# Sums of up-projection weights on VectorE in place of adding DMAs, in a one-core hybrid encoder layer

## The chip, the core and the metric

The kernel runs on one core of one Trainium2 chip. Times are device microseconds (us) of one execution; lower is better. A core has TensorE (PE) for matmuls, VectorE (DVE), ScalarE (ACT), GpSimd (POOL), which here issues DMAs that add into their destination, and SyncE (SP), which issues the plain loads. Each of these works through its own list of instructions in order, and semaphores hold an instruction back until what it needs is there.

## What is computed

One post-norm layer on x of 512 x 1024 floats: a token-mixing part (state-space branch, dilated attention, gates) and a channel part. The change lies in the channel part:

```
h = layer_norm(alpha * h + mix, ln1_g, ln1_b)
f = jnp.square(jax.nn.relu(h @ w_up)) @ w_down      # w_up 1024 x 4096, w_down 4096 x 1024
h = layer_norm(alpha * h + f, ln2_g, ln2_b)
```

## The kernel before

Every fp32 matmul is done as three matmuls on split operands: a high part (a cast to fp32r by ACT) and a low part (the source minus the high part, by DVE). So each block of weights passes from HBM into a raw tile, then ACT writes its high part, then DVE its low part, and PE multiplies.

The channel part has 32 column blocks of `w_up`, each 128 columns wide, in four chunks of eight, and `w_down` is consumed by chunk. The first eight blocks are done plainly. The other 24 are done as **12 pairs**, numbered n = 0 to 11 (`PAIRS`, line 1029), while the down projection of the chunk before is multiplied between them. The big loop at line 1265 has three **passes**, c = 0, 1, 2, of four pairs each (n = 4c + q) and seven products of the down projection. A pair is a Strassen-like scheme with seven instead of eight quarter products; it needs sums of weights. The pair's two blocks lie in raw tiles r0 and r1 (named `pr`, three buffers in the tag `wraw`, which SP loads). K0 and K1 are the halves of a tile's 1024 columns. `pair_prep(n, e)` makes the operands in four steps:

- e = 0, operand tile pa: r0 as it stands (two quarter products, into the PSUM banks x and y);
- e = 1, operand tile pb: T1 = r0K0 + r1K0 and T2 = T1 + r1K1, kept in the two halves of pb (banks z and x);
- e = 2, operand tile pc: r1, whose K0 half has become r1K0 + r1K1 (banks x and z);
- e = 3, operand tile pd: r0K1 + T2 (bank x).

The four sums are made in place in r0 and r1, by four adding DMAs of 256 KB that POOL issues (lines 1063, 1067, 1068, 1070). pa, pb, pc and pd rotate through three slots (`slot`), two of them in one tag and one in another; so pa of the next pair waits until PE has done with this pair's pb. `pair_load` for r1 of pair n + 1 is issued once r1 of pair n has had its last reader, which is the low part of pc; r0 likewise after pd.

PE's order is written by hand (`manual_schedule`, lines 1264 to 1300). Within a pair it is: x and y from pa, then z and x from pb, then x and z from pc, then x from pd, twelve matmuls each. The products of the down projection stand between them, 24 matmuls each, named `ps_p` by line 148 to 150. For the first pair of a pass (q = 0) pb follows pa at once. For the others half a product stands between pa and pb, and its other half between pb and pc:

```
if q == 0:
    up_seg(n, 1)
    pair_prep(n, 3)
pr = product(c, SEQ[2 * q], ops)
next(pr)
if q:
    up_seg(n, 1)
    pair_prep(n, 3)
```

The operands of a product are ah, al (the activations) and ch, cl (the weights, two tiles each, in two buffers per tag). The down weights are summed too, by four adding DMAs of 1 MB per pass (`wq<-wq`, line 1171), which POOL issues from the same list. The one that the second pair of a pass needs (its first product, `SEQ[2]`) starts only when the operands of the product before have been split, since it adds into the tile that they were split from.

The order on ACT, DVE, POOL and SP isn't written by hand: a list scheduler sets it when the program is built, from the dependences and its own costs. So the order after the change is that scheduler's, too.

Of the kernel before, what the change touches and what calls it, by code (L numbers as in the profile page):

```python
# [13 lines left out]
ALU = mybir.AluOpType  # L14
# [26 lines left out]
def f32(ap):  # L41
    return ap.bitcast(F32)
# [3 lines left out]
def hybrid_layer_kernel(ctx: ExitStack, tc: tile.TileContext, t: dict, out: bass.AP):  # L46
    nc = tc.nc
    act, dve, pool, pe, dma = nc.scalar, nc.vector, nc.gpsimd, nc.tensor, nc.sync
# [984 lines left out]
    def pair_load(n, j):  # L1033
        if n < len(PAIRS):
            ch, b = PAIRS[n]
            raw_w[n, j] = wp.tile([P, 1024], F32, name=f"pr{n}_{j}", tag="wraw", bufs=3)
            dma.dma_start(raw_w[n, j], t["w_up"][ch * 8 + b + j])
# [3 lines left out]
    def slot(name):  # L1041
        s_ = slot_n[0] % 3
        slot_n[0] += 1
        if s_ < 2:
            return [wp.tile([P, 1024], F32R, name=f"{name}{x}", tag=f"w{x}", bufs=2) for x in "hl"]
        return [fp.tile([P, 1024], F32R, name=f"{name}{x}", tag=f"x{x}", bufs=1) for x in "hl"]

    def wsplit(h, l, src):
        act.copy(h, src)
        dve.tensor_sub(l, src, f32(h))  # L1050

    K0, K1 = slice(0, 512), slice(512, 1024)

    def pair_prep(n, e):

        if n >= len(PAIRS):
            return
        r0, r1 = raw_w[n, 0], raw_w.get((n, 1))
        if e == 0:
            h, l = slot(f"pa{n}")  # L1060
            wsplit(h, l, r0)
            op_w[n, "B11"], op_w[n, "B21"] = (h, l, K0), (h, l, K1)
            pool.dma_start(r0[:, K0], r1[:, K0], accum_op=ALU.add)
        elif e == 1:
            h, l = slot(f"pb{n}")
            wsplit(h[:, K0], l[:, K0], r0[:, K0])
            pool.dma_start(r1[:, K0], r1[:, K1], accum_op=ALU.add)
            pool.dma_start(r0[:, K0], r1[:, K1], accum_op=ALU.add)
            wsplit(h[:, K1], l[:, K1], r0[:, K0])
            pool.dma_start(r0[:, K1], r0[:, K0], accum_op=ALU.add)  # L1070
            op_w[n, "T1"], op_w[n, "T2"] = (h, l, K0), (h, l, K1)
        elif e == 2:
            h, l = slot(f"pc{n}")
            wsplit(h, l, r1)
            op_w[n, "T3"], op_w[n, "B22"] = (h, l, K0), (h, l, K1)
            pair_load(n + 1, 1)
        else:
            h, l = slot(f"pd{n}")
            wsplit(h[:, K0], l[:, K0], r0[:, K1])
            op_w[n, "T4"] = (h, l, K0)  # L1080
            pair_load(n + 2, 0)
# [162 lines left out]
    for b in range(NU, 8):  # L1244
        if b == 4:
            hf_ctx.close()
            qp = wq_ctx.enter_context(tc.tile_pool(name="qp", bufs=1, side="right", reuse_waits="tile"))
            load_quarters(0)
        up_block(0, b)
        if b == 2:  # L1250
            s3 = act_sums()
        if b == 7:
            act_split("S3", s3)
            pair_load(0, 0)
            pair_load(0, 1)
            pair_load(1, 0)
            pair_prep(0, 0)
            pair_prep(0, 1)
# [5 lines left out]
    with tc.manual_schedule(engines={mybir.EngineType.PE}):  # L1264
        for c in range(3):
            for q in range(4):
                n = c * 4 + q
                if q:
                    up_seg(n - 1, 3)
                up_seg(n, 0)  # L1270
                pair_prep(n, 2)
                if q == 0:
                    up_seg(n, 1)
# [148 lines left out]
```

## Time and profile before

| | us |
|---|---|
| median of 3 timed runs (1026.52 to 1027.15) | 1026.8 |
| the profiled execution's own time | 1027.21 |
| its span, first to last instruction | 1025.4 |
| PE busy, share of the span | 991.2, 97% |
| DVE busy | 758.8, 74% |
| ACT busy | 589.8, 58% |
| POOL busy | 103.0, 10% |
| mean granted TensorE clock, of 1 | 0.985 |

The profile names an instruction by its line in the kernel, its engine, its operation and the tiles that it writes and reads (`out<-in`). In a timeline the first column is the start, the second the time from the first start to the last end, `xN` the number of instructions merged, and what stands in brackets is the idle time of the engine just before and what ended it. The time between the starts of two instructions that follow each other without a wait is a little shorter than one instruction's duration, as the next one enters while the last one drains. In a table of stretches, `PEclk` is the clock that TensorE was granted. PE's busy time is an average over the whole kernel: 97% says that few microseconds are without a matmul, not that the matmuls ran at full clock.

### The profile page before, as it was taken

What the parts mean: (1) busy time and instruction counts of PE and PEld (TensorE: products, weight loads), DVE (VectorE), ACT (ScalarE), POOL (GpSimd) and SP (SyncE); (2) the same over time, 40 slices, a digit from 0 to 9 for tenths busy, and PEclk for the clock granted to TensorE, in tenths of its full rate; (3) what the DMA queues carried; (4) which work ended last, traced back from release to release, by engine and by line L of the source; (5) the groups of instructions that cost most, each with busy time, mean ns of one, the idle gap of its engine ahead of it and who ended that gap; (6) DMA issues with size and microseconds to landing.
All of it is one profiled execution on the core that took longest, in us unless ns stands there. A gap on an engine that the chain in (4) does not pass through costs nothing.

```text
span 1025.4 us, 14690 instructions
## 1 busy us (share of the span) xinstructions
PE 991.2 (97%) x5399; PEld 841.0 (82%) x5399; DVE 758.8 (74%) x1176; ACT 589.8 (58%) x1127; POOL 103.0 (10%) x110
## 2 busy tenths in 40 slices
PE   9999999999999999999999999998999799789997
PEld 7888888888887887788788888887898689679986
DVE  4396998689988998984984483964885777668756
ACT  4454795579757975965763443364655456455630
POOL 0000100110021003011000000001212211221100
PEclk9999999999999999999999999999999899889999
DMA  6445475226633772665752386066777886875522
GB/s 237 149 143 151 130 219 186 93 98 197 195 107 106 223 212 76 200 194 169 262 155 90 104 272 231 23 206 143 151 209 186 178 191 180 194 160 135 136 92 82
DMA packets 61992, 165.67 MB, mean 162 GB/s; under 512 B 8032, under 2 KB 9312, under 8 KB 60128
## 3 DMA queue, kind: packets, MB, share of 16 engines
q1 hardware_dynamic: 53136, 139.30, 42.2%
q0 software_dynamic: 8640, 25.17, 13.4%
q8 instruction: 42, 0.69, 0.3%
q10 hardware_dynamic: 144, 0.26, 0.1%
q14 instruction: 30, 0.25, 0.1%
HBM read 128.25 MB, written 11.30 MB: 136 GB/s over the span
## 4 chain that ended last, share of the span: by engine, by line
PE 75%; DMA 12%; DVE 6%; issue 4%; ACT 2%; POOL 1%; SPq 0%; DVEq 0%; POOLq 0%; ACTq 0%
PE ps_pa L138 9%; PE ps_z L138 9%; PE ps_x L138 9%; PE ps_g L138 7%; DMA pr<-pr 6%; DMA wq<-wq 4%; PE ps_q L138 3%; PE ps_k L138 3%; PE ps_x L1089 2%; PE ps_u L138 2%; PE ps_B L138 2%; PE ps_yo L529 2%; PE ps_C L138 2%; DMA pr<-in_w_up_dram 2%; PE ps_p L149 1%
## 5 line engine op out<-in xcount | busy, mean ns | idle before, releaser
L108 DVE TENSOR_TENSOR wl<-wraw,wh 128x1024 fp32r<-128x1024 f32 (+1 forms) x117 | 144.1, 1236 | 104.8 <-ACT wh L107 79.5
L107 ACT CAST wh<-wraw 128x1024 fp32r<-128x1024 f32 (+1 forms) x117 | 120.9, 1037 | 105.7 <-PE ps_vb L150 16.5
L148 PE MATMUL ps_p<-ch,ah 128*128 128x512 f32 x168 | 67.8, 404 | 3.0 <-ACT ch L1183 3.0
L149 PE MATMUL ps_p<-cl,ah 128*128 128x512 f32 x168 | 68.0, 405 | 2.6 <-DVE cl L1184 2.6
L1184 DVE TENSOR_TENSOR cl<-wq,ch 128x1024 fp32r<-128x1024 f32 x42 | 51.0, 1221 | 22.4 <-ACT ch L1183 22.4
L150 PE MATMUL ps_p<-ch,al 128*128 128x512 f32 x168 | 67.0, 399 | 0.0
L1183 ACT CAST ch<-wq 128x1024 fp32r<-128x1024 f32 x42 | 43.4, 1043 | 16.2 <-DMA wq<-wq 10.1
L138 PE MATMUL ps_pa<-yh,wh 128*128 128x512 f32 x128 | 51.7, 404 | 0.0
L138 PE MATMUL ps_g<-xh,wh 128*128 128x512 f32 x128 | 51.5, 402 | 0.0
L138 PE MATMUL ps_z<-xh,wh 128*128 128x512 f32 x128 | 50.7, 396 | 0.0
L138 PE MATMUL ps_x<-xh,wh 128*128 128x512 f32 x128 | 50.5, 394 | 0.0
L138 PE MATMUL ps_z<-xl,wh 128*128 128x512 f32 x128 | 49.9, 390 | 0.0
L138 PE MATMUL ps_g<-xl,wh 128*128 128x512 f32 x128 | 49.9, 390 | 0.0
L138 PE MATMUL ps_x<-xl,wh 128*128 128x512 f32 x128 | 49.9, 390 | 0.0
L498 ACT ACTIVATE U<-bc,acr 128x128 f32<-128x128 f32 x128 | 42.4, 391 | 11.1 <-DMA bc<-dr_acr 7.5
L138 PE MATMUL ps_pa<-yl,wh 128*128 128x512 f32 x128 | 48.4, 393 | 0.0
L317 DVE SCALAR_TENSOR_TENSOR acc<-ps_x,vec,acc 128x510 f32<-128x510 f32 (+1 forms) x64 | 47.6, 743 | 0.8 <-ACT acc L315 0.3
L500 DVE SCALAR_TENSOR_TENSOR U<-bc,acr,U 128x128 f32<-128x128 f32 x128 | 42.0, 364 | 0.6 <-ACT U L498 0.6
L138 PE MATMUL ps_u<-ht,wh 128*128 128x512 f32 (+1 forms) x160 | 41.7, 348 | 0.2 <-ACT ht L955 0.2
L504 ACT ACTIVATE G<-cb,tok 128x128 f32<-128x128 f32 x128 | 41.8, 391 | 0.0
L148 PEld LDWEIGHTS ps_p<-ch,ah 128*128 128x128 f32 x168 | 32.9, 196 | 9.8 <-ACT ch L1183 3.7
L149 PEld LDWEIGHTS ps_p<-cl,ah 128*128 128x128 f32 x168 | 32.8, 195 | 9.7 <-DVE cl L1184 3.9
(752 smaller groups left out, 2679.9 us busy)
## 6 DMA issues: line engine op xcount, KB each, us to landing
wraw<-in_w_in_dram SPq DMA_DIRECT2D x68, 512.0 KB, 3.6
bc<-dr_acr SPq DMA_DIRECT2D x64, 256.0 KB, 4.6
wq<-in_w_dn_dram SPq DMA_DIRECT2D x24, 512.0 KB, 4.7
wq<-wq POOLq DMA_DIRECT2D x12, 1024.0 KB, 7.9
pr<-in_w_up_dram SPq DMA_DIRECT2D x24, 512.0 KB, 4.9
pr<-pr POOLq DMA_DIRECT2D x48, 256.0 KB, 3.5
be<-dr_ear SPq DMA_DIRECT2D x32, 256.0 KB, 5.4
wraw<-in_w_ps_dram SPq DMA_DIRECT2D x16, 512.0 KB, 3.7
```

What stands on the lines that cost most here:

```text
L107: act.copy(h[:, :width], r[:, :width])
L108: dve.tensor_sub(l[:, :width], r[:, :width], f32(h[:, :width]))
L138: ins = pe.matmul(ps, l, r, start=(first and n == 0), stop=(last and n == len(seq) - 1))
L148: pe.matmul(ps, lh, rh, start=(first and i == 0), stop=False)
L149: pe.matmul(ps, lh, rl, start=False, stop=False)
L150: ins = pe.matmul(ps, ll, rh, start=False, stop=(last and i == n - 1))
L317: dve.scalar_tensor_tensor(acc[:, o0:o1], ps[:, i0:i1], w(k), acc[:, o0:o1], op0=ALU.mult, op1=ALU.add)
L498: act.activation(U[:, ch(c)], bb[:, ch(c)], AF.Identity, bias=acr[:, c, 32 + h:33 + h])
L500: dve.scalar_tensor_tensor(U[:, ch(c)], bf[:, ch(c)], acr[:, c, h:h + 1], U[:, ch(c)], op0=ALU.subtract, op1=ALU.min)
L504: act.activation(G1[:, ch(c)], cb[0][:, c, :], AF.Copy, scale=tok[:, c, h:h + 1])
L1183: act.copy(h, w[:, j, :])
L1184: dve.tensor_sub(l, w[:, j, :], f32(h))
```

## The change

The four adding DMAs of a pair become four VectorE additions of 128 x 512 floats, in place, on the same halves; and the split of pb, which called `wsplit` for each half, is written out so that the additions stand between the casts and the subtractions. Loads, matmuls, the adding DMAs of the down weights and the order on PE stay as they are.

```
         if e == 0:
             h, l = slot(f"pa{n}")
             wsplit(h, l, r0)
             op_w[n, "B11"], op_w[n, "B21"] = (h, l, K0), (h, l, K1)
-            pool.dma_start(r0[:, K0], r1[:, K0], accum_op=ALU.add)
         elif e == 1:
             h, l = slot(f"pb{n}")
-            wsplit(h[:, K0], l[:, K0], r0[:, K0])
-            pool.dma_start(r1[:, K0], r1[:, K1], accum_op=ALU.add)
-            pool.dma_start(r0[:, K0], r1[:, K1], accum_op=ALU.add)
-            wsplit(h[:, K1], l[:, K1], r0[:, K0])
-            pool.dma_start(r0[:, K1], r0[:, K0], accum_op=ALU.add)
+            dve.tensor_add(r0[:, K0], r0[:, K0], r1[:, K0])
+            act.copy(h[:, K0], r0[:, K0])
+            dve.tensor_add(r1[:, K0], r1[:, K0], r1[:, K1])
+            dve.tensor_sub(l[:, K0], r0[:, K0], f32(h[:, K0]))
+            dve.tensor_add(r0[:, K0], r0[:, K0], r1[:, K1])
+            act.copy(h[:, K1], r0[:, K0])
+            dve.tensor_add(r0[:, K1], r0[:, K1], r0[:, K0])
+            dve.tensor_sub(l[:, K1], r0[:, K0], f32(h[:, K1]))
             op_w[n, "T1"], op_w[n, "T2"] = (h, l, K0), (h, l, K1)
```

The first place is DVE's list at pair 0, the first pair of the first pass. `pa0`, `pb0` and `pc0` are its operands (h the high part, l the low part), `pr_0` and `pr_1` its raw tiles; line 1015 splits activations, line 1169 (now 1171) sums activations for the down projection, line 1178 (now 1180) splits them, and line 1120 (now 1122) takes bank y out of PSUM. Before:

```order
L1050 TENSOR_TENSOR pa0l<-pr_0_6741,pa0h 128x1024
L1015 TENSOR_TENSOR ht<-s_6553,ht 128x4x256
L1050 TENSOR_TENSOR pb0l<-pr_0_6741,pb0h 128x512
L1169 TENSOR_TENSOR r_0_6470<-r_0_6470,r_1_6616 128x4x256
L1120 TENSOR_TENSOR r_1_6777<-ps_y_6791,v_0_6804 128x256
L1050 TENSOR_TENSOR pc0l<-pr_1_6743,pc0h 128x1024
L1178 TENSOR_TENSOR al_6882<-r_0_6470,ah_6881 128x1024
L1050 TENSOR_TENSOR pb0l<-pr_0_6741,pb0h 128x512
```

And of the change, at the same place on DVE:

```order
L1050 TENSOR_TENSOR pa0l<-pr_0_6741,pa0h 128x1024
L1065 TENSOR_TENSOR pr_0_6741<-pr_0_6741,pr_1_6743 128x512
L1067 TENSOR_TENSOR pr_1_6743<-pr_1_6743 128x512
L1015 TENSOR_TENSOR ht<-s_6553,ht 128x4x256
L1050 TENSOR_TENSOR pc0l<-pr_1_6743,pc0h 128x1024
L1068 TENSOR_TENSOR pb0l<-pr_0_6741,pb0h 128x512
L1171 TENSOR_TENSOR r_0_6470<-r_0_6470,r_1_6616 128x4x256
L1069 TENSOR_TENSOR pr_0_6741<-pr_0_6741,pr_1_6743 128x512
L1122 TENSOR_TENSOR r_1_6777<-ps_y_6791,v_0_6804 128x256
L1071 TENSOR_TENSOR pr_0_6741<-pr_0_6741 128x512
L1180 TENSOR_TENSOR al_6882<-r_0_6470,ah_6881 128x1024
L1072 TENSOR_TENSOR pb0l<-pr_0_6741,pb0h 128x512
```

The four additions (L1065, L1067, L1069, L1071) stand between the splits, and the split of pc has moved ahead of both halves of pb.

The second place is DVE's list in the second pair of the second pass (pair 5), from its pc to the second half of the next product's weights, `cl_7927`. `pr_0_7669` and `pr_1_7851` are the raw tiles of pair 6, `v` and `h` are sums of the output. Before:

```order
L1050 TENSOR_TENSOR pc5l<-pr_1_7634,pc5h 128x1024
L1050 TENSOR_TENSOR pd5l<-pr_0_7501,pd5h 128x512
L1184 TENSOR_TENSOR cl_7923<-wq_01_7553,ch_7922 128x1024
L1050 TENSOR_TENSOR pa6l<-pr_0_7669,pa6h 128x1024
L1234 TENSOR_TENSOR v_0_7697<-v_0_7697,ps_p_3_7853 128x512
L1223 TENSOR_TENSOR h_0_6038<-h_0_6038,v_0_7697 128x512
L1234 TENSOR_TENSOR v_1_7700<-v_1_7700,ps_p_4_7854 128x512
L1178 TENSOR_TENSOR al_7997<-r_0_7209,ah_7996 128x1024
L1223 TENSOR_TENSOR h_1_6039<-h_1_6039,v_1_7700 128x512
L1184 TENSOR_TENSOR cl_7927<-wq_01_7553,ch_7926 128x1024
```

And of the change:

```order
L1050 TENSOR_TENSOR pc5l<-pr_1_7634,pc5h 128x1024
L1050 TENSOR_TENSOR pd5l<-pr_0_7501,pd5h 128x512
L1180 TENSOR_TENSOR al_7919<-r_0_7209,ah_7918 128x1024
L1186 TENSOR_TENSOR cl_7923<-wq_01_7552,ch_7922 128x1024
L1050 TENSOR_TENSOR pa6l<-pr_0_7669,pa6h 128x1024
L1236 TENSOR_TENSOR v_0_7697<-v_0_7697,ps_p_3_7853 128x512
L1065 TENSOR_TENSOR pr_0_7669<-pr_0_7669,pr_1_7851 128x512
L1225 TENSOR_TENSOR h_0_6038<-h_0_6038,v_0_7697 128x512
L1236 TENSOR_TENSOR v_1_7700<-v_1_7700,ps_p_4_7854 128x512
L1137 SCALAR_TENSOR_TENSOR r_1_7599<-ps_x_7817,v_5_7892 128x256
L1225 TENSOR_TENSOR h_1_6039<-h_1_6039,v_1_7700 128x512
L1186 TENSOR_TENSOR cl_7927<-wq_01_7552,ch_7926 128x1024
```

L1065, the first sum of pair 6, which reads the raw tile `pr_1_7851`, now stands in DVE's list ahead of `cl_7927`. The first and third pass have L1065 of pairs 2 and 10 at the same place.

The third place is POOL's list at pair 4, the first pair of the second pass. Before:

```order
L1063 DMA pr_0_7293<-pr_1_7452 128x512
L1067 DMA pr_1_7452<-pr_1_7452 128x512
L1171 DMA wq_00_7550<-wq_01_7553 128x2048
L1068 DMA pr_0_7293<-pr_1_7452 128x512
L1171 DMA wq_01_7553<-wq_11_7556 128x2048
L1070 DMA pr_0_7293<-pr_0_7293 128x512
```

And of the change, where nothing but adding DMAs of the down weights is left from here to the end of the kernel:

```order
L1173 DMA wq_00_7549<-wq_01_7552 128x2048
L1173 DMA wq_01_7552<-wq_11_7555 128x2048
L1173 DMA wq_00_7549<-wq_11_7555 128x2048
L1173 DMA wq_00_7549<-wq_10_7558 128x2048
L1173 DMA wq_00_8371<-wq_01_8374 128x2048
L1173 DMA wq_01_8374<-wq_11_8377 128x2048
```

The adding DMAs of the raw tiles are gone from it, and those of the down weights have no others between them.

## The prediction

> **What bounds the kernel now.** I read the page first, then PE's waits in the stage of the 12 pairs, then PE's timeline there. The stage runs from the first matmul of pair 0 to the last of pair 11:
>
> ```profile
> 704.30:974.30 270.00, 247.66 (x1514) 223.28 (x1513) 193.04 (x239) 149.34 (x226) 49.11 (x57) 0.95 0.71 169
> ```
>
> PE is busy 247.7 of 270.0 us at a mean granted clock of 0.95, DVE 193.0, ACT 149.3. So PE bounds it, but neither its gaps nor its slow clock are small. The gaps:
>
> ```profile
> PE ps_x L1089 <- ACT pb4h L1049: 7.0, 1, 7.0
> PE ps_x L1089 <- ACT pb8h L1049: 6.8, 1, 6.8
> PE ps_p L148 <- ACT ch L1183: 3.0, 3, 1.8
> PE ps_x L1089 <- ACT pb0h L1049: 3.0, 1, 3.0
> PE ps_p L149 <- DVE cl L1184: 2.6, 4, 0.8
> ```
>
> Two kinds: pb, the tile of weight sums, comes late in the first pair of each pass (pairs 0, 4, 8); and the weights of a product (ch, cl) come late three times. The timeline gives the place and whole cost of each, with the slow clock after it:
>
> ```profile
> 707.17 1.12 PE L1089 MATMUL ps_z<-S,pb0h 128*128 128x256 f32 x8
> 711.74 2.08 PE L1089 MATMUL ps_x<-S,pb0h 128*128 128x256 f32 x8 [2.97 <-ACT pb0h L1049]
> 714.47 0.46 PE L148 MATMUL ps_p<-ch,ah 128*128 128x512 f32 x1
> 722.90 0.40 PE L148 MATMUL ps_p<-ch,ah 128*128 128x512 f32 x1
> 728.36 1.12 PE L1089 MATMUL ps_x<-ht,pd0h 128*128 128x256 f32 x8
> 731.24 1.12 PE L1089 MATMUL ps_y<-ht,pa1h 128*128 128x256 f32 x8
> 737.09 1.11 PE L1089 MATMUL ps_z<-S,pb1h 128*128 128x256 f32 x8
> 792.34 1.12 PE L1089 MATMUL ps_z<-S,pb4h 128*128 128x256 f32 x8
> 810.60 1.12 PE L1089 MATMUL ps_x<-ht,pc4h 128*128 128x256 f32 x8
> 821.82 1.12 PE L1089 MATMUL ps_y<-ht,pa5h 128*128 128x256 f32 x8
> 828.27 1.11 PE L1089 MATMUL ps_z<-S,pb5h 128*128 128x256 f32 x8
> 883.24 1.12 PE L1089 MATMUL ps_z<-S,pb8h 128*128 128x256 f32 x8
> 900.35 1.11 PE L1089 MATMUL ps_x<-ht,pc8h 128*128 128x256 f32 x8
> 910.70 1.12 PE L1089 MATMUL ps_x<-ht,pa9h 128*128 128x256 f32 x8
> 912.14 1.12 PE L1089 MATMUL ps_y<-ht,pa9h 128*128 128x256 f32 x8
> 921.61 1.65 PE L1089 MATMUL ps_z<-S,pb9h 128*128 128x256 f32 x8
> ```
>
> Undisturbed, a quarter product takes 1.44 us (910.70 to 912.14), a product 5.46 (722.90 to 728.36), half of one 2.73. Three passes hold 84 quarter products and 21 products: 84 x 1.44 + 21 x 5.46 = 235.6 us. So 34.4 of the 270.0 are lost, and 32.4 of these can be placed:
>
> - pair 0: from z at 707.17 the product should start two quarter products later, 710.05; it starts at 714.47: **4.4** lost;
> - pair 4: from z, two quarter products and one product, 800.68; pc4 starts at 810.60: **9.9**; pair 8 likewise, 891.58 against 900.35: **8.8**;
> - pairs 1, 5, 9: from y, one quarter product and half a product, 735.41, 825.99, 916.31; pb starts at 737.09, 828.27, 921.61: **1.7, 2.3, 5.3**.
>
> Why pb4 is so late stands in the timelines of POOL and ACT:
>
> ```profile
> 791.20 1.16 POOL L1171 DMA_DIRECT2D wq<-wq  x1
> 791.80 1.45 POOL L1068 DMA_DIRECT2D pr<-pr  x1
> 800.25 0.62 ACT L1049 CAST pb4h<-pr 128x512 fp32r<-128x512 f32 x1 [1.88 <-DMA pr<-pr]
> ```
>
> The sum that pb4's second half needs (L1068, second row) is issued right behind a 1 MB sum of down weights (first row), and is there for ACT only at 800.25. Pair 8 has the same list.
>
> **What goes, and what comes.** 48 adding DMAs go:
>
> ```profile
> pr<-pr POOLq DMA_DIRECT2D x48, 256.0 KB, 3.5
> wq<-wq POOLq DMA_DIRECT2D x12, 1024.0 KB, 7.9
> ```
>
> The second row, which mixes 12 of the larger DMAs, stays. In place of the first come 48 additions on DVE. The nearest row is an in-place sum of the same shape; the next instruction tells the spacing, and two rows of 1024 columns likewise:
>
> ```profile
> 742.62 0.69 DVE L1223 TENSOR_TENSOR h<-h,v 128x512 f32<-128x512 f32 x1
> 743.23 0.68 DVE L1234 TENSOR_TENSOR v<-v,ps_p 128x512 f32<-128x512 f32 x1
> 718.24 1.21 DVE L1050 TENSOR_TENSOR pa1l<-pr,pa1h 128x1024 fp32r<-128x1024 f32 x1
> 719.38 1.21 DVE L1184 TENSOR_TENSOR cl<-wq,ch 128x1024 fp32r<-128x1024 f32 x1
> ```
>
> So 0.61 us of DVE each (0.69 where the next instruction needs the result), 1.14 for 1024 columns. 48 x 0.61 = 29 us: DVE goes from 193 to 222 busy us, in a stage that cannot be shorter than 235.6. It fits, with little slack, so DVE's order decides.
>
> *Pair 0.* I walk DVE's new list with these durations; a cast takes ACT 0.62 us for 512 columns (first row here), and about 1.05 for 1024 (half of the 2.00 us of the row at pairs 1, 5, 9 below):
>
> ```profile
> L1049 ACT CAST pb0h<-pr x2: 615/618/621, 705.4 to 711.1; 128x512 fp32r<-128x512 f32 x2
> 703.66 1.23 DVE L1015 TENSOR_TENSOR ht<-s,ht 128x1024 fp32r<-128x1024 f32 x1 [1.81 <-PE ps_u L138]
> ```
>
> L1015 waits for PE until 703.66 as before. Then pc0l to 706.0, pb0l's first half 706.6, L1171 707.8, L1069 708.4. ACT casts a 1024-column tile for the next product first (707.8 to 708.8), then pb0h's second half, to 709.4. PE wants it at 708.61: 0.8 us late. DVE reaches pb0l's second half behind L1122, L1071 and L1180, at 710.35, done 711.0; PE wants it 0.96 us after 709.4: 0.7 late. So 1.5 remain of 4.4, and gaps this short leave the clock alone (below). Gain **2.9**.
>
> *Pairs 4 and 8.* No adding DMA is in the chain any more; what holds pb4 is its slot, which pc3 gives back when PE has used it, at T. Then ACT casts pb4's first half (T + 0.7), and DVE does its split (T + 1.4), L1069, L1071, pc4's split and pb4's second half: T + 4.5. PE does pd3 and pa4 (T + 4.3) and z, and wants that last piece at T + 6.7. So it is 2 us ahead. Next late is the first product's al: its source is squared by ACT only after pd3's matmuls (T + 2.7), cast by T + 4.2, and al is behind L1171 in DVE's list, done T + 7.0; PE wants it in the product's third matmul, T + 7.65. I leave 0.5 us of loss each: gain **9.4 + 8.3 = 17.7**.
>
> *Pairs 1, 5, 9.* Their loss doesn't come from the sums that go:
>
> ```profile
> 724.36 1.10 POOL L1171 DMA_DIRECT2D wq<-wq  x1
> 732.10 2.00 ACT L1183 CAST ch<-wq 128x1024 fp32r<-128x1024 f32 x2 [2.71 <-DMA wq<-wq]
> 816.29 0.86 POOL L1171 DMA_DIRECT2D wq<-wq  x1 [1.77 <-DVE cl L1184]
> ```
>
> The 1 MB sum of down weights starts when DVE has split the weights of the product before: at 724.36, 4.4 us after the end of the product that began at 714.47; and it takes 7.7. In the second pass it starts 5.7 after the product's end (816.29 against 810.60, where pc4 follows), behind a late pd4. By my walk it starts 4 to 5 after in each pass. So 1.7, 2.0, 2.0 remain: gain 0.0 + 0.3 + 3.3 = **3.6**. Were the 1 MB DMA faster without the others, more would go; but before the first sum of raw tiles one took 8.7:
>
> ```profile
> wq<-wq POOLq DMA_DIRECT2D x1, 1024.0 KB, 8.7
> ```
>
> The Trainium skill (DMA: Bandwidth & Descriptors, Anatomy of one DMA — SWDGE (gpsimd) path) gives about 2.0 us plus the bytes over 436 GB/s, an estimate of 4.4 us for 1 MB; with that the three waits would vanish and the sum be some 5 us better. The trace, with 7.9 in the median, doesn't agree.
>
> **A wait is added.** L1065 of the next pair stands in DVE's list, and waits for the load of raw tile r1, which SP issues when pc's split is done. In pairs 1, 5, 9 a 1 MB sum is in flight then, and the load takes
>
> ```profile
> pr<-in_w_up_dram SPq DMA_DIRECT2D x2, 512.0 KB, 7.3
> ```
>
> DVE comes to L1065 4.6 us after pc's split (pd 0.61, al, cl, pa 1.14 each, v 0.61), and waits 2.7. Queued behind it are h, v, L1137, h and cl of the next product's second half: done 7.3 + 0.69 + 4 sums (2.2) + 1.22 = 11.4 us after the load's issue. For pair 5 I count from t, when the first late cl is done. DVE: second cl 1.14, L1069, L1122, L1071, pb's split, pc's split: issue at t + 4.75, cl at t + 16.2. PE: rest of half a product, z and x, the other half, pc, half a product: its first matmul with cl at t + 13.95. So 2.2 us of stall, for pair 9 too; at pair 1 the list has L1069 and L1071 ahead of the late cl, so 0.8. Loss **5.2**. In other pairs no 1 MB sum is in flight at that time and the load is ahead. Bounds: 0, if the load lands within 4.6, and 9.4, if it takes as long as the 8.7 of the 1 MB sum that it shares the DMA engines with (1.4 more each). I take 7.3, as it was measured at the same place.
>
> The rest of DVE's lateness (cl of the second product of pairs 2, 6, 10 is within 0.3 us of PE by the walk): loss **1.0**.
>
> Sum: 2.9 + 17.7 + 3.6 - 5.2 - 1.0 = 18.0. Own time 1027.2 - 18.0 = **1009.2**; it lies 0.4 above the median of the three runs, so 1009. After the stage nothing changes; the tail moves up as a whole.
>
> **Rivals.**
>
> *The waits that remain halve the clock.* At pair 9 a gap of 1.75 and one of 0.77 did:
>
> ```profile
> 732.00:734.00 2.00, 1.33 (x8) 1.00 0.46 82
> 916.00:918.00 2.00, 1.25 (x3) 0.50 0.38 72
> ```
>
> Pair 1's shorter ones (first row) didn't. If pairs 1, 5 and 9 each lose 5.3 as pair 9 did, and not 5.7 together, the time is 1009.2 + 10.2 = 1019. The Trainium skill (TensorE: Matmul & The Clock Gate, What's actually happening) has the clock halved after an idle window of about 3.4 us that runs freely; by that a gap near 2 us would be safe, and 1009 stand. The trace agrees only in part: at pair 9 the clock fell within 2.6 us.
>
> *The waits go.* With the small sums off the DMA queue the loads land within 4.6, L1065 waits for nothing, and DVE's slack is enough: 1009.2 - 5.2 - 1.0, and some 3 of the 5.7 at pairs 1, 5, 9: 1000.
>
> *Slower.* DVE becomes the bound in the middle pairs, where sums of the output wait for PE at the head of its list and an addition and the next cl stand behind them. DVE is idle 77 of the 270 us now. From 270 - 222 = 48 us of idle that stay on, the kernel is slower; halfway to all of it, 62, the stage takes 284 and the kernel 1041; with 45 to 50, there is no difference. Against it: PE stands still for 16.8 us at the three late pb (second view), DVE's list is then empty of work but for splits that wait for the same sums, and the sums of the middle pairs held DVE up in the same way through ACT's casts.
>
> **Chances.** Forecast (1003 to 1014) 0.55; halved clock (1014 to 1022) 0.18; waits go (996 to 1003) 0.18; no difference 0.04; slower 0.05. The range 1000 to 1018 takes in the first and most of the next two, some 0.8. A measurement of this kernel tells 0.2%, 2 us, from no change: faster 0.91, same 0.04, slower 0.05.
>
> **What would show it.** PE's waits for pb4h and pb8h gone and for pb0h under 1 us; the granted clock of the stage near 1.00; POOL issuing only sums of down weights there; DVE busy about 222 us of a stage of 252. A wait of DVE L1065 for `in_w_up`, followed by a wait of PE for cl in pairs 1, 5, 9, confirms the added wait. If PE waits for pb or pc in middle pairs, DVE is the bound and I am wrong.

## The result, and the profile after

| | before | after |
|---|---|---|
| median, us (6 runs each, side by side) | 1027.02 (1026.52 to 1027.66) | 999.02 (998.61 to 999.38) |
| profiled execution's own time, span | 1027.21, 1025.4 | 999.2, 997.4 |
| DVE busy, POOL busy | 758.8, 103.0 | 784.6, 61.8 |
| mean granted TensorE clock | 0.985 | 0.998 |

The change is faster: ratio 0.9727, 95% interval 0.9714 to 0.9739; 28.0 us. The forecast was 1009, range 1000 to 1018: the sign and the main mechanism were right, the gain was 10 us larger than forecast and 1 us beyond the range's end.

The stage of the 12 pairs in the table of stretches of the changed kernel, from its first matmul to its last (columns: span; busy us of PE, its weight loads, DVE, ACT, POOL; granted clock; DMA share; GB/s):

```profile
703.90:946.10 242.20, 238.05 (x1514) 215.30 (x1513) 217.49 (x285) 149.77 (x226) 8.56 (x10) 1.00 0.50 137
```

270.0 us have become 242.2, so 27.8 of the 28.0 us are here. DVE is busy 24.5 us more (the prediction had 29), and the clock is 1.00. The view of PE's waits over the same stage has three rows left:

```profile
PE ps_p L149 <- DVE cl L1186: 3.0, 6, 0.8
PE ps_x L1091 <- ACT pb0h L1070: 0.6, 1, 0.6
PE ps_x L1091 <- DVE pb0l L1072: 0.5, 1, 0.5
```

The waits for pb4h and pb8h are gone, and that for pb0h is 0.6. PE's timeline at pairs 4 and 5:

```profile
788.37 1.12 PE L1091 MATMUL ps_z<-S,pb4h 128*128 128x256 f32 x8
...
796.72 1.11 PE L1091 MATMUL ps_x<-ht,pc4h 128*128 128x256 f32 x8
...
798.15 1.12 PE L1091 MATMUL ps_z<-S,pc4h 128*128 128x256 f32 x8
...
807.93 1.12 PE L1091 MATMUL ps_y<-ht,pa5h 128*128 128x256 f32 x8
...
812.65 1.11 PE L1091 MATMUL ps_z<-S,pb5h 128*128 128x256 f32 x8
...
825.06 0.50 PE L149 MATMUL ps_p<-cl,ah 128*128 128x512 f32 x1 [0.78 <-DVE cl L1186]
```

From pb4's z to pc4 it is 8.35 us, two quarter products and a product (8.34): nothing is lost where 9.9 us were. From pa5's y to pb5 it is 4.72 against 4.17 undisturbed: 0.55 lost, before 2.3. The last row is one of the three small waits that the change adds, at pairs 1, 5 and 9; the other two are 0.33 and 0.63.

### The profile page after: what moved, and what is told of

Its sections match the earlier page's. It is cut to its first block, busy times and chain, and to the rows that moved or that the text cites. A ratio compares the mean times of both kernels' runs of the same rounds, so it can differ in the third digit from the quotient of the medians.

```text
span 997.4 us, 14586 instructions
## 1 busy us (share of the span) xinstructions
PE 982.3 (98%) x5399; PEld 833.3 (84%) x5399; DVE 784.6 (79%) x1224; ACT 591.7 (59%) x1127; POOL 61.8 (6%) x62
## 4 chain that ended last, share of the span: by engine, by line
PE 72%; issue 11%; DVE 8%; DMA 7%; ACT 1%; POOL 0%; DVEq 0%; SPq 0%; POOLq 0%; ACTq 0%
PE ps_pa L138 9%; PE ps_z L138 9%; PE ps_x L138 9%; PE ps_g L138 7%; DMA wq<-wq 4%; PE ps_q L138 3%; PE ps_k L138 3%; PE ps_B L138 2%; PE ps_yo L529 2%; DMA pr<-in_w_up_dram 2%; PE ps_C L138 2%; PE ps_d L149 1%; PE ps_d L148 1%; PE ps_d L150 1%; DVE cl L1186 1%
## 5 line engine op out<-in xcount | busy, mean ns | idle before, releaser
L148 PE MATMUL ps_p<-ch,ah 128*128 128x512 f32 x168 | 65.8, 391 | 0.0
L1186 DVE TENSOR_TENSOR cl<-wq,ch 128x1024 fp32r<-128x1024 f32 x42 | 51.0, 1222 | 12.1 <-ACT ch L1185 11.9
L150 PEld LDWEIGHTS ps_p<-ch,al 128*128 128x128 f32 x168 | 31.6, 188 | 6.6
```

The source lines that it names most:

```text
L148: pe.matmul(ps, lh, rh, start=(first and i == 0), stop=False)
L150: ins = pe.matmul(ps, ll, rh, start=False, stop=(last and i == n - 1))
L1186: dve.tensor_sub(l, w[:, j, :], f32(h))
```

## The experiments

All were timed beside the kernel before on the same chip; chips differ by about 1 us.

| kernel | us, median | before beside it | ratio, 95% interval |
|---|---|---|---|
| first: VectorE sums in pairs 0, 4, 8 | 1009.43 | 1026.31 | 0.9838 (0.9823 to 0.9853) |
| middle: in the other nine pairs | 1026.26 | 1026.31 | 1.0003 (0.9991 to 1.0015) |
| order: DMAs, one 1 MB sum moved | 1028.93 | 1026.31 | 1.0029 (1.0015 to 1.0043) |
| none: the sums left out | 997.07 | 1026.31 | 0.9720 (0.9705 to 0.9734) |
| pairs01: VectorE sums in pairs 0, 1, 4, 5, 8, 9 | 999.69 | 1025.49 | 0.9745 (0.9723 to 0.9768) |
| only1: all but pairs 1, 5, 9 | 1008.69 | 1025.49 | 0.9827 (0.9809 to 0.9846) |
| behind_cl: L1065 behind cl | 996.70 | 1025.49 | 0.9719 (0.9702 to 0.9737) |
| twice: each addition twice | 1012.57 | 1025.49 | 0.9872 (0.9855 to 0.9889) |
| after_again: the changed kernel | 999.68 | 1025.87 | 0.9744 (0.9731 to 0.9758) |
| second_sum: a 1 MB sum on VectorE too | 997.23 | 1025.87 | 0.9722 (0.9709 to 0.9735) |
| both: second_sum with behind_cl | 997.46 | 1025.87 | 0.9724 (0.9711 to 0.9737) |
| gpsimd: sums by GpSimd's arithmetic | 1011.94 | 1025.87 | 0.9866 (0.9851 to 0.9881) |
| after_third: the changed kernel | 998.72 | 1026.93 | 0.9728 (0.9706 to 0.9750) |
| behind_cl_2: as behind_cl | 997.21 | 1026.93 | 0.9712 (0.9690 to 0.9734) |

### The two halves of the change, and the order of the list

The theory was that the gain sits where the first pair of a pass hung on small sums queued behind a 1 MB sum; the rival was that 48 small transfers slow everything a little.

```
+            if not (n % 4 == 0):
+                pool.dma_start(r0[:, K0], r1[:, K0], accum_op=ALU.add)
         elif e == 1:
             h, l = slot(f"pb{n}")
-            dve.tensor_add(r0[:, K0], r0[:, K0], r1[:, K0])
...
+            if n % 4 == 0:
+                dve.tensor_add(r0[:, K0], r0[:, K0], r1[:, K0])
...
+            else:
+                wsplit(h[:, K0], l[:, K0], r0[:, K0])
+                pool.dma_start(r1[:, K0], r1[:, K1], accum_op=ALU.add)
...
```

This is first, against the changed kernel: the `else` holds the lines of before. Middle has the two conditions the other way round.

> The sums of weights on VectorE in pairs 0, 4 and 8 alone (12 of 48); the other nine pairs sum by adding DMAs as before. Theory of the chain (the gain sits where pb of a pass's first pair hung on sums queued behind a 1 MB sum): PE's losses at pairs 0, 4, 8 fall from 4.4 + 9.9 + 8.8 = 23.1 us to the 1.6 us of the changed kernel, so about 21.5 us of the 28 come with this part alone, 1005 us, and between 1002 and 1006 if the waits of pairs 5 and 9 shrink with them. Rival, contention (48 small transfers slow every 1 MB sum and every load, so the gain is spread over all twelve pairs): a quarter to a half of 28 us, 1013 to 1020 us.

> The opposite part alone: sums on VectorE in the nine middle pairs (36 of 48), adding DMAs as before in pairs 0, 4 and 8. Theory of the chain: PE's waits for pb4h and pb8h stay at about 7 us each and the clock still falls behind them; what can be gained is the losses at pairs 1, 5, 9 (9.3 us before, 2.3 in the changed kernel) less 1.7 us for the added wait, so 1021 to 1028 us. Rival, contention: half to three quarters of 28 us, 1006 to 1013 us.

First gave 16.9 us, middle none, the whole 28: **11 us come only when both halves are there.** The theory of the chain was right that the middle pairs bring nothing alone, and wrong that the first pairs alone bring 21.5. What took the rest is in POOL's and ACT's timelines of first, at pairs 4 and 5 (L1182 issues the 1 MB sums, L1064, L1078, L1079 and L1081 the small ones of pair 5):

```profile
793.62 0.86 POOL L1182 DMA_DIRECT2D wq<-wq  x1 [7.18 <-DMA wq<-wq]
795.17 0.86 POOL L1064 DMA_DIRECT2D pr<-pr  x1 [0.70 <-DVE pa5l L1050]
...
803.58 0.86 POOL L1078 DMA_DIRECT2D pr<-pr  x1 [7.55 <-DMA pr<-pr]
804.12 1.21 POOL L1182 DMA_DIRECT2D wq<-wq  x1
...
811.95 1.99 ACT L1194 CAST ch<-wq 128x1024 fp32r<-128x1024 f32 x2 [5.62 <-DMA wq<-wq]
```

and in PE's timeline of first:

```profile
798.39 1.12 PE L1100 MATMUL ps_z<-S,pc4h 128*128 128x256 f32 x8
...
813.05 0.79 PE L148 MATMUL ps_p<-ch,ah 128*128 128x512 f32 x1 [3.27 <-ACT ch L1194]
...
819.16 1.26 PE L1100 MATMUL ps_z<-S,pb5h 128*128 128x256 f32 x8
```

Pair 5's first small sum, issued at 795.17 behind the 1 MB sum of 793.62, lands some 8 us later. The second small sum waits for it, and the next 1 MB sum stands behind that in POOL's list: 804.12. In the changed kernel it is issued at 800.77, as soon as cl is split. Counted from the end of the product before it, that is 3.1 us later, and the transfer takes 7.8 us in place of 6.8: the place in the list is the larger part of the lateness, a slower transfer the smaller. So ch is late, PE waits 3.27 us, and its next matmul takes 0.79 in place of 0.50. From pc4's z to pb5 it is 20.77 us, in the changed kernel 14.50.

Middle shows the other direction, in the timelines of POOL and DVE at the same pairs (L1081 is the last small sum of pair 4):

```profile
797.29 0.86 POOL L1182 DMA_DIRECT2D wq<-wq  x1 [5.99 <-DMA wq<-wq]
798.58 0.86 POOL L1081 DMA_DIRECT2D pr<-pr  x1 [0.42 <-DMA pr<-pr]
...
808.38 0.69 DVE L1050 TENSOR_TENSOR pd4l<-pr,pd4h 128x512 fp32r<-128x512 f32 x1 [3.84 <-ACT pd4h L1049]
...
809.59 1.22 DVE L1195 TENSOR_TENSOR cl<-wq,ch 128x1024 fp32r<-128x1024 f32 x1
...
815.18 0.86 POOL L1182 DMA_DIRECT2D wq<-wq  x1 [15.74 <-DVE cl L1195]
```

A small sum behind a 1 MB sum makes pd4 late; DVE waits 3.84 us for it with cl behind it in its list; and cl is what the next 1 MB sum waits for, which is issued at 815.18. PE's wait at pair 4 was 1.9 us shorter than before (5.1 against 7.0), and pb5 came at 828.61, before at 828.27: the gain was given back within a pair. In the list of transfers of this stretch the last small sum took

```profile
pr<-pr POOLq DMA_DIRECT2D x1, 256.0 KB, 9.1
```

where the median before was 3.5. So what held the kernel was a single list in which small and 1 MB sums wait behind each other, in both directions. The Trainium skill (DMA: Bandwidth & Descriptors, SWDGE vs HWDGE vs iDMA) says that only one queue is allocated to the DMAs that GpSimd issues; the 9.1 us are in line with it.

The next kernel is the one before with one DMA moved; `last_sum` is the fourth small sum of the pair. For this, the call that prepares the first pb of the next pass is also written ahead of the one that prepares the product (not shown).

```
-            pool.dma_start(w, wadd, accum_op=ALU.add)
+            if ch and p == 5:
+                with tc.issue_after(last_sum[0].ins):
+                    pool.dma_start(w, wadd, accum_op=ALU.add)
+            else:
+                pool.dma_start(w, wadd, accum_op=ALU.add)
```

> All sums by adding DMAs as before; the one edit is that in passes 2 and 3 the 1 MB sum of down weights that stood ahead of the fourth sum of pairs 4 and 8 is issued behind it. Theory of the chain (what hurt was the place in the queue behind 1 MB, not the adding DMA as such): the last sum of pb4 and pb8 lands some 4 us earlier, PE waits about 3 us there in place of 7 and the clock falls less; 8 to 12 us gained, 1015 to 1019 us, less up to 3 us if the 1 MB sum is then late for its own product. Rival (four adding DMAs of 3.5 us one behind the other are too slow in any order): under 3 us gained, 1024 to 1027 us.

Two rows of PE's waits tell the outcome:

```profile
PE ps_p L148 <- ACT ch L1188: 11.6, 2, 6.4
PE ps_x L1090 <- ACT pb4h L1050: 3.1, 1, 3.1
```

The wait for pb4h fell from 7.0 to 3.1 us, as the theory said. The 1 MB sum then came late for its own product, 6.4 us at pair 5, which was priced at up to 3: the time missed the forecast by 10 us. This order of the list doesn't serve both, and no other was tried; the theory needed the two directions.

### Which pairs' sums matter

Two kernels were made for that theory of the list: the condition `n % 4 == 0` of first becomes `n % 4 < 2` (pairs01) and `n % 4 != 1` (only1).

> Sums on VectorE in the first two pairs of each pass (0, 1, 4, 5, 8, 9), adding DMAs as before in the other six (24 DMAs stay). Theory of the list (GpSimd issues its DMAs in order and they land in order; the small sums of pairs 0, 4, 8 stand behind a 1 MB sum, those of pairs 1, 5, 9 stand in front of the next one, and the small sums of the other pairs stand beside nothing that is awaited): nearly all of the 28 us, 998 to 1001 us. Rival, contention (each small transfer costs its share wherever it is): about half to three quarters of the 28 us, 1006 to 1013 us.

> The complement: sums on VectorE in nine pairs, adding DMAs as before in pairs 1, 5 and 9 alone (12 DMAs). Theory of the list: the 1 MB sum of the third product waits again behind the sums of pair 5 and 9, PE waits some 3 us for ch there as with VectorE sums in pairs 0, 4, 8 alone, and the clock falls behind that; most of the 10 to 11 us by which the two halves of the change miss the whole are lost here, 1006 to 1010 us. Rival, contention: a quarter of the small transfers, at most a quarter of 28 us lost, spread out: 1001 to 1006 us.

Both came out inside the forecast of the list and outside that of contention. With 24 small DMAs still in the program, pairs01 takes 999.69 us, as much as the whole change; with only 12 of them, in pairs 1, 5 and 9, only1 takes 1008.69. POOL's timeline of only1 repeats that of first:

```profile
793.02 0.86 POOL L1182 DMA_DIRECT2D wq<-wq  x1 [7.19 <-DMA wq<-wq]
794.58 0.86 POOL L1064 DMA_DIRECT2D pr<-pr  x1 [0.70 <-DVE pa5l L1050]
803.12 0.86 POOL L1078 DMA_DIRECT2D pr<-pr  x1 [7.68 <-DMA pr<-pr]
803.66 1.21 POOL L1182 DMA_DIRECT2D wq<-wq  x1
```

In pairs01 the same 1 MB sum is issued at 801.25, as soon as cl is split, with nothing ahead of it:

```profile
801.25 0.86 POOL L1182 DMA_DIRECT2D wq<-wq  x1 [7.01 <-DVE cl L1195]
```

So the place decides, not the count. Half of the change's additions, those of pairs 2, 3, 6, 7, 10 and 11, bring nothing that shows beside the spread of pairs01's runs (997.48 to 1002.39).

### What the additions cost on VectorE

`none` deletes the four `dve.tensor_add`; `twice` adds behind each

```
             dve.tensor_add(r0[:, K0], r0[:, K0], r1[:, K0])
+            dve.tensor_add(spare, r0[:, K0], r1[:, K0])
```

> The changed kernel with the four sums of each pair left out (the middle product's weights are then the raw tiles), so that neither VectorE nor a DMA does them. It prices what the 48 additions still cost. Theory: only the losses that stand in their way go, 1.6 us at pair 0 in part and the 1.7 us behind the added wait at L1065; 995.5 to 998 us. Rival (VectorE's order has become the bound, 29 us of additions are felt): 985 to 994 us.

> The changed kernel with each of the 48 additions followed by a second one of the same operands into a spare tile that nobody reads: 48 x 0.61 = 29 us more of VectorE, no change of any value. Theory (VectorE has slack; 222 of 242 us would become 251, more than the stage has, so some must be paid): at least 251 - 242 = 9 us, 1008 to 1018 us. Rival, VectorE's order was already what bounds the middle pairs: all 29 us paid, 1025 us or more. If there is far more slack than the busy times say: 999 to 1005 us.

Without the additions the kernel takes 997.07 us, the changed one 999.02, on two chips; as ratios to the kernel before beside each it is 0.9720 against 0.9727, and the intervals overlap. So the additions, some 29 us of VectorE work, cost 2 us at most. As much work again costs 13.6 us by the times (1012.57 against 999.02) and 15 by the ratios. Both times lie inside the forecasts of the theory. VectorE had slack for about half of a second helping, and then became late in many small places, as PE's waits in twice show:

```profile
PE ps_x L1096 <- ACT pb6h L1074: 1.9, 1, 1.9
PE ps_x L1096 <- ACT pb10h L1074: 1.9, 1, 1.9
PE ps_x L1096 <- ACT pb0h L1074: 1.5, 1, 1.5
PE ps_x L1096 <- DVE pb8l L1077: 1.1, 1, 1.1
```

### The added wait at L1065

`cl_of[7]` is the last split of the weights (cl) of the product that runs beside pairs 2, 6 and 10's preparation.

```
+            if n % 4 == 2:
+                with tc.issue_after(cl_of[7].ins):
+                    dve.tensor_add(r0[:, K0], r0[:, K0], r1[:, K0])
+            else:
+                dve.tensor_add(r0[:, K0], r0[:, K0], r1[:, K0])
```

> The changed kernel, with the first addition (L1065) of pairs 2, 6 and 10 put in VectorE's list behind the split of the second product's weights (cl) instead of ahead of it, so that nothing that PE wants soon is queued behind the wait for the load of raw weights. Theory: PE's waits for cl in the second half of that product (0.33 + 0.78 + 0.63 = 1.7 us) go, 997 to 998 us. As I had priced that wait (5.2 us), 994 us. Rival (cl is late for another reason, or the additions are now late for pb): 999 us or more.

> The changed kernel as yardstick in the same rounds: 998 to 1000.5 us.

> First addition of pairs 2, 6, 10 behind cl, in the same rounds as the changed kernel. If the wait at L1065 costs what PE's three waits for cl in the changed kernel's profile say, 1.2 to 1.7 us less than the yardstick; if it costs the 5.2 us that I forecast, 5 less; if it is hidden, within 0.5.

In the same rounds the changed kernel took 998.72 us (998.34 to 999.41) and behind_cl_2 997.21 (996.51 to 997.73): 1.5 us, about what PE's waits said (2.7 in the changed kernel's profile of these rounds became 1.5), and not the 5.2 that I had forecast. Behind_cl, the same kernel on another chip and with no changed kernel in its rounds, took 996.70, forecast 997 to 998. PE's wait for cl in behind_cl_2:

```profile
PE ps_p L149 <- DVE cl L1191: 1.5, 3, 0.8
```

The three that remain are those of pairs 1, 5 and 9, where the 1 MB sum is late.

### One more sum off the list

```
-            pool.dma_start(w, wadd, accum_op=ALU.add)
+            if p == 6:
+                for j in range(2):
+                    dve.tensor_add(w[:, j, :], w[:, j, :], wadd[:, j, :])
+            else:
+                pool.dma_start(w, wadd, accum_op=ALU.add)
```

> The changed kernel once more, on the chip and in the rounds of the three kernels beside it, as their yardstick: 998 to 1000 us by every theory.

> The changed kernel, with one of the four 1 MB sums of down weights of each pass also on VectorE: the one that PE waits for at pairs 1, 5 and 9 (two additions of 1024 columns each in place of one DMA). Theory (PE waits there because that DMA takes some 7 us from a late issue, and VectorE has room): the waits of 0.8 + 0.55 + 0.9 = 2.3 us go, 996.5 to 997.5 us; with the load of raw weights no longer beside a 1 MB DMA, the wait at L1065 shrinks too and with it up to 1.7 us: down to 995. Rival (6 x 1.14 = 7 us more of VectorE at the place where its list is fullest, so that pb or pc of these pairs is late): 999 to 1004 us.

> That second sum on VectorE together with the first addition of pairs 2, 6, 10 behind the split of the second product's weights: by the theory both small waits go, 995 to 996 us; by the rival of a full VectorE list 998 to 1004 us.

Second_sum took 997.23 us (996.90 to 997.79) against 999.68 (999.09 to 1000.37) for the changed kernel in the same rounds: 2.4 us. All six waits for cl are gone, those behind L1065 too, but not for the reason forecast: the load of raw weights still has a 1 MB DMA beside it. The timelines of POOL, SP and DVE at pair 5:

```profile
807.87 0.86 POOL L1177 DMA_DIRECT2D wq<-wq  x1 [16.20 <-DVE cl L1190]
...
810.88 3.27 SPq L1037 DMA_DIRECT2D pr<-in_w_up_dram  x2
...
817.78 1.21 DVE L1190 TENSOR_TENSOR cl<-wq,ch 128x1024 fp32r<-128x1024 f32 x1
...
828.66 0.68 DVE L1065 TENSOR_TENSOR pr<-pr,pr 128x512 f32<-128x512 f32 x1
```

The first load issued at 810.88 takes 6.1 us, and the 1 MB sum, issued at 807.87, 7.9. The scheduler's new list has L1065 of pair 6 behind the cl that PE waited for (the third row), some 12 us after the load has landed. So it waits for nothing and holds nothing up; but pb hangs on it, and PE now waits for pb6h and pb10h.

```profile
PE ps_x L1091 <- ACT pb6h L1070: 1.0, 1, 1.0
PE ps_x L1091 <- ACT pb10h L1070: 1.0, 1, 1.0
```

The kernel named both has the same two waits and the same time, as there was nothing left at L1065 to move. Its forecast of 995 to 996 missed. Behind_cl_2, second_sum and `both` are faster than the changed kernel beside them, by 1.5, 2.4 and 2.2 us; the runs of each don't overlap those of the changed kernel, while the intervals of the two ratios to the kernel before do.

### Another engine

The four `dve.tensor_add` become `pool.tensor_add`.

> The four sums of each pair as additions on GpSimd's own arithmetic in place of VectorE: no small DMA and no addition on VectorE, but GpSimd issues the 1 MB sums from the same list. An addition of 512 columns took GpSimd 1.3 to 1.8 us earlier in the program. Theory of the list: the chain of pb in a pass's first pair is longer by about four times 0.9 us than on VectorE and was 2 us ahead there, so some 2 us are lost at each of pairs 0, 4 and 8, and the 1 MB sum of pairs 1, 5, 9 waits behind additions that wait for loads: 1003 to 1012 us. Rival (any engine but the DMA queue will do): 998 to 1001 us.

It is slower than the changed kernel by 12 us, within the forecast, but in part for a reason that was not in it. In POOL's timeline the 1 MB sum of pair 5 does not wait behind additions:

```profile
807.67 0.87 POOL L1173 DMA_DIRECT2D wq<-wq  x1 [4.86 <-DVE cl L1186]
```

GpSimd stood idle ahead of it until a late cl was split, and likewise at pairs 1 and 9 (3.71 and 4.85 us). The groups of DVE for two instructions that the change doesn't touch, in the changed kernel:

```profile
L1186 DVE TENSOR_TENSOR cl<-wq,ch 128x1024 fp32r<-128x1024 f32 x40 | 48.6, 1222 | 11.2 <-ACT ch L1185 11.0
L1225 DVE TENSOR_TENSOR h<-h,v 128x512 f32<-128x512 f32 x20 | 13.4, 686 | 0.0
```

and with the sums on GpSimd:

```profile
L1186 DVE TENSOR_TENSOR cl<-wq,ch 128x1024 fp32r<-128x1024 f32 x40 | 56.8, 1425 | 16.3 <-ACT ch L1185 16.2
L1225 DVE TENSOR_TENSOR h<-h,v 128x512 f32<-128x512 f32 x20 | 17.7, 901 | 0.1
```

The same instructions take 17 and 31% longer, PE's waits for cl rise from 3.0 to 4.8 us, and waits for ch, of which the changed kernel has none, add 3.9. How much of the 12 us comes from VectorE's longer instructions, and how much from GpSimd's own additions, these runs do not separate.

## Why the prediction was right in kind and 10 us short

The sum by its own terms; what is lost is measured in the profiled execution as the prediction did it (start of a tile's matmuls against undisturbed spacing):

| term | forecast | measured |
|---|---|---|
| pair 0 | +2.9 (1.5 remain) | +2.8 (1.6 remain) |
| pairs 4, 8 | +17.7 (0.5 remain each) | +18.7 (none) |
| pairs 1, 5, 9 | +3.6 (1.7, 2.0, 2.0 remain) | +7.0 (0.8, 0.55, 0.9) |
| wait at L1065 | -5.2 (0.8, 2.2, 2.2) | -2.6 (0.6, 1.1, 0.9) |
| other lateness of DVE | -1.0 | 0 |
| not placed (2.0 before) | 0 | +1.9 |
| outside the stage | 0 | +0.2 |
| sum | 18.0 | 28.0 |

So the sum fell short in two terms above all, pairs 1, 5, 9 by 3.4 us and the wait at L1065 by 2.6. The rest is 1.9 that the prediction had not placed and let stand without a reason, and 1.0 each that it left at pairs 4 and 8 and put to other lateness of DVE. PE's waits at L1065 (0.33, 0.78, 0.63) are shorter than the loss there, since idle time counts from the end of the last matmul, 0.39 us behind its start, where without a wait the next one starts after 0.23; and the first one behind a wait takes longer, too.

**What bounds the kernel** was read rightly: PE, with its losses at three late pb and the slow clock behind them. The walk of pair 0, through DVE's new list with durations of the profile, was right to 0.1 us.

**Pairs 1, 5 and 9: the step that failed.** The term had the 1 MB sum take 7.7 us and so left 5.7 us of loss; 2.2 were left. "Their loss doesn't come from the sums that go" was also wrong as a cause, at pairs 5 and 9. In the profile of before the 1 MB sum of pair 5 waited for a late cl behind a late pd4, as the prediction itself notes, and pd4 was late through the last small sum of pair 4. The rows of POOL and DVE in the kernel before:

```profile
799.24 0.86 POOL L1171 DMA_DIRECT2D wq<-wq  x1 [5.99 <-DMA wq<-wq]
800.51 0.86 POOL L1070 DMA_DIRECT2D pr<-pr  x1 [0.42 <-DMA pr<-pr]
...
810.34 0.69 DVE L1050 TENSOR_TENSOR pd4l<-pr,pd4h 128x512 fp32r<-128x512 f32 x1 [3.87 <-ACT pd4h L1049]
```

It is the same chain as in middle, and pair 9 has it too. At pair 1 the sentence held: in order, with all small sums of pass 1 as before, the loss there is 0.8. Only1 shows that with that repaired the small sums of pairs 1, 5, 9 would still hold this 1 MB sum back: 1008.69 us. The sum did not inherit that error, as it let the issue come 4 to 5 us after the product before. It came 4.3, 4.05 and 4.05 after, at the low end, and the DMA took 6.8, 6.8 and 7.2 us, where the term had used pair 1's 7.7 for all three. POOL's rows in the changed kernel, for pairs 1, 5 and 9:

```profile
721.03 0.86 POOL L1173 DMA_DIRECT2D wq<-wq  x1 [28.39 <-DVE cl L1186]
...
800.77 0.85 POOL L1173 DMA_DIRECT2D wq<-wq  x1 [7.20 <-DVE cl L1186]
...
880.98 0.86 POOL L1173 DMA_DIRECT2D wq<-wq  x1 [7.19 <-DVE cl L1186]
```

Small DMAs beside it do not alone decide how long it takes: in order, where pass 1 is as before, pair 1's 1 MB sum took 6.8 us, and in middle, without small sums there, those of pairs 1, 5, 9 took 6.8, 6.8 and 7.9; in first, with them, those of pairs 5 and 9 took 7.8. Before, pair 5's took 6.9. One sample, 7.7, was taken from a spread, and what sets the spread stays open.

**The wait at L1065: right mechanism, mis-sized: 2.6 us in place of 5.2.** DVE waits there as forecast, and cl behind it is late:

```profile
821.04 0.69 DVE L1065 TENSOR_TENSOR pr<-pr,pr 128x512 f32<-128x512 f32 x1 [2.10 <-DMA pr<-in_w_up_dram]
...
823.78 1.22 DVE L1186 TENSOR_TENSOR cl<-wq,ch 128x1024 fp32r<-128x1024 f32 x1
```

Counted from t, the end of the first late cl (809.92 here), cl was done at t + 15.1, forecast t + 16.2; PE came to it at t + 14.4, forecast 13.95. The load of r1 took 6.5 us in place of the 7.3 that I took, and was issued 0.3 earlier. A stall that is the difference of two walks of 14 to 16 us carries the errors of both: PE waits 0.78 in place of 2.2. Behind_cl_2 confirms the small price by time, 1.5 us.

**Rivals.** The halved clock at pairs 1, 5, 9 did not come, since those waits stayed under 0.6 us. It is a real threat: in first, order and only1, with waits of 2.7 us and more at this place, the clock did fall. "The waits go", 1000 us, was the nearest in time, but by its own account only half right: DVE still waits at L1065, and the gain lies in smaller prices. "Slower" needed 48 us of idle time on DVE to stay; 24.7 of 242.2 us stayed (242.2 - 217.5), and twice shows that 29 us more would still have been faster than before.

**The range.** Four residual terms (pairs 4 and 8, pairs 1, 5, 9, L1065, other lateness) were each set towards the dearer end of what the rows allowed, and they add. Set to their cheap ends (issue after 4.0 and 6.9 us for the 1 MB sum, 1.2 less than pair 1's 4.4 and 7.7, which leaves 0.5 in place of 1.7 there, and as much at pairs 5 and 9; nothing at L1065, the bound that the prediction gave; nothing at pairs 4 and 8 or for other lateness) they add 4.2 + 5.2 + 1.0 + 1.0 = 11.4 to the gain: 997.8. The range should have reached there.

## What to carry to other kernels

Before a DMA that adds is priced by its own duration, look at what stands ahead of and behind it in its list: here half of the transfers cost nothing and the other half 28 us. A chain through such a list can hold the critical path in several places in turn, so the parts of a change need not add up (16.9 and 0 gave 28), and a place that looks independent in the profile may only be masked by an earlier one. Where several small residues are uncertain, a range must contain their joint cheap end as well as their dear one.

## What was not expected of the hardware

- Additions on GpSimd lengthen VectorE's instructions beside them: 1222 to 1425 ns and 686 to 901 ns in the mean (rows above). The Trainium skill (Trainium Architecture — The Big Picture, What this means for kernel authors) names a pair of ports that these two engines share and lock against each other; the rows agree for VectorE, and GpSimd's own additions, of 1.3 to 2.2 us in the same trace, are in line with it; in which way they hold each other up the rows do not show.
- The 1 MB adding DMA took 6.8 to 9.7 us over these kernels: the longest in order, right behind a small one, but 9.4 also in behind_cl_2, which has no small one, and 6.8 with and without small ones near.
- TensorE fell to a lower clock in a wait of 2.7 us for ch. At pair 9 of gpsimd waits of 1.97 and 0.77 us were enough (0.50 behind them), while at pair 9 of first a wait of 3.24 ended with the clock still at 1.00, and it fell some 2 us later: the length of a wait alone does not tell. The table of stretches of only1 around the first:

```profile
812.00:816.00 4.00, 2.97 (x6) 2.07 (x7) 3.30 (x4) 3.99 (x7) 1.65 (x2) 0.51 0.41 74
```

- The profile of after_again shows a granted clock of 0.95 in every stretch, this one among them, where the first profile of the same kernel shows 1.00, and yet the usual time, 1000.37 us. The column is to be compared between stretches of one profile first.

```profile
788.00:870.00 82.00, 81.42 (x525) 73.96 (x524) 74.64 (x98) 52.29 (x81) 3.42 (x4) 0.95 0.60 161
```
